# The first pair of tiles of a ConvFFN in direct block products, and a third room for split weights

## The chip, the cores and the metric

The kernel runs on one core of a Trainium2 chip. Its engines are called PE (matmuls), DVE, ACT and POOL (elementwise work) and SP, whose queue issues the transfers. The metric is the device time of one execution, in microseconds (us).

## What is computed

Two layers of a diffusion backbone over 1024 latent tokens and 256 context tokens of width 1024, in fp32. Each layer is a mixer (layer 0 a gated MLP beside a gated DeltaNet, layer 1 latent attention) and then a ConvFFN; only the latter concerns us. Layer 0 runs it on all 1280 tokens, layer 1 on the 1024 latent ones.

```python
def conv_ffn(h, w_up, conv_w, w_down):
    g, u = jnp.split(dwconv(h @ w_up, conv_w), 2, axis=-1)
    return (jax.nn.silu(g) * u) @ w_down
...
lat = lat + g2 * conv_ffn(modulate(rms_norm(lat, norm2_g[i]), sh2, sc2),
                          ffn_w_up[i], ffn_conv_w[i], ffn_w_down[i])
```

Here w_up is 1024 x 5632 and w_down 2816 x 1024.

## The kernel before

Every fp32 operand is split into a rounded part and a rest (h and l in the names): line 125 casts the rounded part on POOL, line 132 subtracts on DVE, and some operands are cast on ACT (line 123). A product of two split operands is three matmuls, h by h, h by l and l by h (lines 407 to 409 in `prod`, 588 to 590 in the down pass). A scheduler orders each engine's instructions when the kernel is built, on a timeline of its own; on the chip each engine takes them strictly in that order, with semaphore waits.

**The up pass** (`ffn_up`) goes over 22 pairs of tiles: tile ci of the gate columns and tile ci of the up columns of w_up, 128 wide each. The 1024 latent tokens make two halves of 512 columns, the width of 1024 two halves of four 128-row blocks. A pair is thus a 2 x 2 by 2 x 2 block product, and it is done in seven products of 12 matmuls with 512 columns (a scheme after Strassen and Winograd) in place of eight. They need B11 and B21 (the first token half), T1 (B12 - B11), B22, T2, T3 and T4 (sums of all four blocks), and S0 to S3, sums of weights that POOL makes (`sums`) and ACT and DVE split (`part`). `operands` makes the B and T blocks in two pieces of 256 columns (`ops[0]` and `ops[1]`). In layer 0 a pair also has 48 matmuls of 256 columns on the context tokens (`context`, bank upc).

The second token half comes late: its last 256 columns are normed (`last`) while the first pair runs. A norm takes squares, column sums on PE (nsum, line 195), their total (nall, line 216), an inverse root on ACT and DVE (from line 218), the scaling in place (xa), and then the operands of piece 1 (T1l, B22l, T2l and T4l on DVE, line 132). `begin[0]` and `begin[1]` put those steps into the program between the products of pair 0. `late` then gives up the memory of xa, and in layer 0 the sums S are made in it. `fill` (`ada1`, layer 0 alone) draws the next modulation's matmuls (ada, from weights adaw of 512 KB each) in between products.

Each pair ends with a convolution over tokens (`finish`, lines 630 and 632 on DVE), a SiLU on ACT, the product of both on POOL (line 496) and a store to DRAM (act<-y).

**The down pass** (`ffn_down`) goes over chunks of tokens (first one of 512, then three or two of 256), for each over two halves of the output and 11 pairs of w_down's blocks (`pr`; pairs count on through the pass as i, so pair 2 is the third). A pair is 24 matmuls with one split weight wdh, wdl. There are two rooms for these, and three for raw ones. After the matmuls of pair i the program asks for the split of pair i + 1 and the load of pair i + 2. The wh of a pair is written when PE has left its room. DVE also splits the down pass's moving operands (al), and works on the norm of the chunk before (the tail; `tail_rooms` holds its ten tiles).

## Time and profile before

| | us |
|---|---|
| median of 3 runs (lowest, highest) | 3308.62 (3308.61, 3311.64) |
| the profiled execution | 3311.97 |
| its span, first to last instruction | 3310.2 |
| PE busy | 3105.2 (94% of the span) |
| DVE, POOL, ACT busy | 2177.8, 1341.9, 1111.8 |
| up pass of layer 0, from its first product | 847.84 to about 1486 |
| down pass of layer 0 | about 1483 to 1815 |
| up pass of layer 1, from its first product | 2552.10 to about 3010 |
| down pass of layer 1 | about 3009 to 3297 |

PE's mean granted clock was 0.973 of full speed. In the page's 40 slices PE is at 9 tenths or more nearly everywhere; the slices at 8 or less hold the starts of stages. The chain of work that ended last covers a per cent or two of the span and so tells nothing here; the waits of PE by stage do.

### The profile page before, as it was taken

To read this page: it belongs to the slowest core of one execution; us is meant where nothing else is said; L and a number is where in the kernel's file an instruction comes from. 1 tells how busy PE (TensorE), PEld (TensorE's weight loads), DVE (VectorE), ACT (ScalarE), POOL (GpSimd) and SP (SyncE) were. 2 spreads that over 40 slices of the span, in tenths; PEclk is the share of its full clock that TensorE was granted. 3 is DMA by queue.
4 is the path that set the end of the run, shared out by engine and by line. 5 is a ranking of instruction groups with operands and counts; after the bars stand their busy time and mean duration, and the time that the engine had idled before them with its cause. 6 is when DMAs were issued, how large, how long until landed. Compare 5 with 4: busy or idle time off the path is not lost. (4 is left out here: it accounts for less than half of the span.)

```text
span 3310.2 us, 48558 instructions
## 1 busy us (share of the span) xinstructions
PE 3105.2 (94%) x18861; PEld 2587.9 (78%) x18861; DVE 2177.8 (66%) x3259; ACT 1111.8 (34%) x2144; POOL 1341.9 (41%) x1218
## 2 busy tenths in 40 slices
PE   7999899998599999999999999999998699999998
PEld 5667787886477788887899778988976577777887
DVE  6332876567765678885576456666657788887455
ACT  5322233333332333341111245555532333333110
POOL 4234323654533355442344232222135566664243
PEclk9999999999799999999999999999999899999999
DMA  7344946753235422144466231000034122225454
GB/s 250 121 141 133 300 134 207 237 152 120 74 121 163 154 97 74 68 151 158 139 223 216 73 104 47 27 22 22 8 128 153 46 82 77 77 83 197 159 192 146
DMA packets 257958, 419.80 MB, mean 127 GB/s; under 512 B 47024, under 2 KB 163968, under 8 KB 257600
## 3 DMA queue, kind: packets, MB, share of 16 engines
q1 hardware_dynamic: 257728, 416.70, 39.4%
q8 instruction: 149, 2.44, 0.3%
q14 instruction: 81, 0.66, 0.1%
HBM read 335.85 MB, written 80.78 MB: 126 GB/s over the span
## 5 line engine op out<-in xcount | busy, mean ns | idle before, releaser
L588 PE MATMUL dn<-ah,wdh 128*128 128x256 f32 (+1 forms) x1232 | 376.5, 317 | 3.8 <-POOL wdh L125 3.8
L589 PE MATMUL dn<-al,wdh 128*128 128x256 f32 (+1 forms) x1232 | 375.6, 316 | 0.0
L590 PE MATMUL dn<-ah,wdl 128*128 128x256 f32 (+1 forms) x1232 | 331.6, 321 | 22.8 <-DVE wdl L132 22.8
L125 POOL TENSOR_SCALAR wdh<-wdr 128x1024 fp32r<-128x1024 f32 x154 | 182.8, 1187 | 381.9 <-PE dn L589 323.0
L132 DVE TENSOR_TENSOR wdl<-wdr,wdh 128x1024 fp32r<-128x1024 f32 x154 | 196.6, 1280 | 193.6 <-POOL wdh L125 189.8
L125 POOL TENSOR_SCALAR wuh<-wur 128x1024 fp32r<-128x1024 f32 (+1 forms) x142 | 169.5, 1194 | 293.2 <-PE upc L408 118.5
L132 DVE TENSOR_TENSOR wul<-wur,wuh 128x1024 fp32r<-128x1024 f32 (+1 forms) x139 | 197.4, 1422 | 108.1 <-POOL wuh L125 107.7
L588 PEld LDWEIGHTS dn<-ah,wdh 128*128 128x128 f32 x1232 | 237.2, 192 | 23.8 <-issue 4.7
L590 PEld LDWEIGHTS dn<-ah,wdl 128*128 128x128 f32 x1232 | 214.7, 193 | 45.6 <-DVE wdl L132 27.4
L589 PEld LDWEIGHTS dn<-al,wdh 128*128 128x128 f32 x1232 | 236.9, 192 | 15.7 <-issue 0.8
L1675 POOL TENSOR_SCALAR p<-p,rsm 128x1280 f32<-128x1280 f32 x63 | 84.7, 1345 | 325.4 <-DVE rsm L1668 164.9
L630 DVE SCALAR_TENSOR_TENSOR y<-raw,fconv,y 128x1023 f32<-128x1023 f32 (+1 forms) x132 | 172.4, 1334 | 32.9 <-ACT y L419 32.6
L139 PE MATMUL proj<-hh,wih 128*128 128x512 f32 (+1 forms) x512 | 185.5, 364 | 0.0
L141 PE MATMUL proj<-hh,wil 128*128 128x512 f32 (+1 forms) x512 | 178.2, 348 | 1.3 <-DVE wil L132 1.3
L140 PE MATMUL proj<-hl,wih 128*128 128x512 f32 (+1 forms) x512 | 178.7, 350 | 0.6 <-DVE hl L253 0.6
L632 DVE SCALAR_TENSOR_TENSOR y<-raw,fconv,y 128x1023 f32<-128x1023 f32 (+1 forms) x132 | 175.6, 1353 | 0.1
L496 POOL TENSOR_TENSOR y<-y,y 128x1280 f32<-128x1280 f32 (+1 forms) x44 | 125.9, 2860 | 109.8 <-issue 61.9
L392 POOL TENSOR_TENSOR s<-wur 128x512 f32<-128x512 f32 x44 | 77.2, 1755 | 181.8 <-DMA wur<-in_w_up 122.1
L1657 DVE TENSOR_REDUCE mx<-sc 128x1 f32<-128x512 f32 (+1 forms) x192 | 114.6, 597 | 40.2 <-PE sc L1656 37.8
L419 ACT ACTIVATE y<-raw,fconv 128x1280 f32<-128x1280 f32 (+1 forms) x88 | 110.7, 1259 | 82.5 <-DVE raw L422 82.0
L110 ACT ACTIVATE p<-sc,nmx 128x512 f32<-128x512 f32 (+1 forms) x192 | 116.2, 617 | 49.1 <-DVE nmx L1661 48.9
L407 PE MATMUL upb<-T2h,S1h 128*128 128x512 f32 x176 | 70.2, 399 | 49.2 <-ACT S1h L123 26.6
(520 smaller groups left out, 9261.1 us busy)
## 6 DMA issues: line engine op xcount, KB each, us to landing
wdr<-in_w_down SPq DMA_DIRECT2D x154, 512.0 KB, 3.7
adaw<-in_ada_w SPq DMA_DIRECT2D x96, 512.0 KB, 4.1
wur<-in_w_up SPq DMA_DIRECT2D x88, 512.0 KB, 3.6
al<-act SPq DMA_DIRECT2D x20, 1024.0 KB, 6.7
t<-t SPq DMA_DIRECT2D x20, 768.0 KB, 6.3
act<-y SPq DMA_DIRECT2D x22, 640.0 KB, 3.0
wur<-in_w_out SPq DMA_DIRECT2D x24, 512.0 KB, 3.4
act<-y SPq DMA_DIRECT2D x22, 512.0 KB, 2.6
```

The source lines that it names most:

```text
L110: self.nc.scalar.activation(out, in_, func, **kw)
L125: nc.gpsimd.tensor_scalar(dst, src, 1.0, 0.0, op0=ALU.mult, op1=ALU.add)
L132: (self.nc.gpsimd if eng == "pools" else self.nc.vector).tensor_tensor(lo, src, f(hi), ALU.subtract)
L139: nc.tensor.matmul(ps, wh, xh, start=first and i == 0, stop=False)
L140: nc.tensor.matmul(ps, wh, xl, start=False, stop=False)
L141: nc.tensor.matmul(ps, wl, xh, start=False, stop=last and i == n - 1)
L496: nc.gpsimd.tensor_tensor(y[1], y[0], y[1], ALU.mult)
L588: nc.tensor.matmul(pss[o], wh[:, q, :], ah, start=pr == j == 0, stop=False)
L589: nc.tensor.matmul(pss[o], wh[:, q, :], al, start=False, stop=False)
L590: nc.tensor.matmul(pss[o], wl[:, q, :], ah, start=False, stop=pr == npr - 1 and j == 1)
L630: nc.vector.scalar_tensor_tensor(out=y[:, s0 + 1:e], in0=raw[:, s0:e - 1], scalar=w[:, 0:1], in1=y[:, s0 + 1:e], op0=ALU.mult, op1=ALU.add)
L632: nc.vector.scalar_tensor_tensor(out=y[:, s0:e - 1], in0=raw[:, s0 + 1:e], scalar=w[:, 2:3], in1=y[:, s0:e - 1], op0=ALU.mult, op1=ALU.add)
```

## The change

It has two parts, the same in both layers.

1. Pair 0 of the up pass is done without sums of weights. The first token half is W B11 + W B21, the second W B11 + W T1 + W B22, each for the gate and the up tile: 72 matmuls of 512 columns, and 96 of 256, since T1 and B22 are taken in their two pieces. The operand steps stand in three places (`begin[0]` to `begin[2]`), the norm's banks nsum and nall can be the single bank "a" (`ntag`), the weights of pair 1 are loaded at once, the sums and splits of pair 1's weights come right behind, and `fill` begins at pair 1, after one step in place of 16.
2. The down pass has a third room for split weights (pool `ffz`, pairs with i % 3 == 2) and asks for the split of pair i + 2 and the load of pair i + 3. `tail_rooms` has six tiles in place of ten, which makes the space. The pool is allocated after the up pass, behind `ffx`.

```diff
...
@@ -184,7 +185,7 @@

         nc = self.nc
         g = min(4, len(xs))
-        ps = self.bank("nsum")
+        ps = self.bank("nsum", self.ntag)
         last = {i % g: i for i in range(len(xs))}
         made = []

@@ -212,7 +213,7 @@
         part = tmp("pt")
         nc.vector.tensor_copy(part[:32 * g, :cn], ps[:32 * g, :cn])
         yield
-        ps2 = self.bank("nall")
+        ps2 = self.bank("nall", self.ntag)
         nc.tensor.matmul(ps2[:, :cn], self.ones[:32 * g, :], part[:32 * g, :cn], start=True, stop=True)
         m, r, t = tmp("m")[:, :cn], tmp("r")[:, :cn], tmp("t")[:, :cn]
         nc.vector.tensor_scalar(m, ps2[:, :cn], 1.0 / (32 * d), EPS, op0=ALU.mult, op1=ALU.add)
@@ -419,35 +420,76 @@
             nc.scalar.activation(y, raw, AF.Copy, scale=w[:, 1:2])
             self.conv_taps(y, raw, w, segs)

+        def gate(ci):
+
+            y = R["y"]
+            self.act(y[0], y[0], AF.Silu)
+            nc.gpsimd.tensor_tensor(y[1], y[0], y[1], ALU.mult)
+            nc.sync.dma_start(self.dr["a"][ci][:, :n], y[1])
+
+        def rows():
+            R["raw"] = [sp.tile([P, n], F32, tag=f"raw{i}", name=f"raw{i}") for i in range(2)]
+            R["y"] = [sp.tile([P, n], F32, tag=f"y{i}", name=f"y{i}") for i in range(2)]
+            raw = R["raw"]
+            return raw, raw[0][:, h1:h1 + 512], raw[1][:, h1:h1 + 512], v2(raw[0]), v2(raw[1])
+
         add = lambda o, a, b: nc.vector.tensor_tensor(o, a, b, ALU.add)
         B = self.B
+
+
+        steps, fill = fill, None
         load(0)
         weight(0, 0)
         weight(0, 1)
-        for ci in range(FT):
-            first = ci == 0
-            a, b, c, d = [None] * 4
+        load(1)
+        ps = [[self.bank("upa") for half in range(2)] for t in range(2)]
+        prod(ps[0][0], W[0], 0, B["B11"])
+        begin[0]()
+        prod(ps[0][1], W[1], 0, B["B11"])
+        for half in range(2):
+            prod(ps[0][half], W[half], 4, B["B21"], False)
+        for half in range(2):
+            prod(ps[1][half], W[half], 0, B["B11"])
+        e = self.bank("upc") if ctx else None
+        if ctx:
+            for half in range(2):
+                for k2 in range(2):
+                    context(e, half, k2)
+        for i in range(2):
+            cs = slice(256 * i, 256 * i + 256)
+            for half in range(2):
+                prod(ps[1][half][:, cs], W[half], 0, B["T1"], False, cs)
+                prod(ps[1][half][:, cs], W[half], 4, B["B22"], False, cs)
+            begin[1 + i]()
+        weight(1, 0)
+        R["sp"], sp = late()
+        sums(1)
+        for i in (1, 0, 2, 3):
+            part(1, i)
+        raw, g1, u1, g2, u2 = rows()
+        for half, (t1, t2) in enumerate(((g1, g2), (u1, u2))):
+            nc.scalar.copy(t1, ps[0][half])
+            nc.vector.tensor_copy(t2, two(ps[1][half]))
+            if ctx:
+                nc.scalar.copy(raw[half][:, :ctx], e[:, 256 * half:256 * half + 256])
+            finish(0, half)
+        weight(1, 1)
+        gate(0)
+        fill = steps
+        for ci in range(1, FT):
+            first = ci == 1
             e = self.bank("upc") if ctx else None
             a = self.bank("upa")
             prod(a, W[0], 0, B["B11"])
             if first:
-                begin[0]()
                 if ctx:
                     for half in range(2):
                         for k2 in range(2):
                             context(e, half, k2)
                 a2 = self.bank("up2")
                 prod(a2, W[0], 4, B["B21"])
-                begin[1]()
-                R["sp"], sp = late()
-                sums(0)
-                for i in (1, 0, 2, 3):
-                    part(0, i)
             load(ci + 1)
-            R["raw"] = [sp.tile([P, n], F32, tag=f"raw{i}", name=f"raw{i}") for i in range(2)]
-            R["y"] = [sp.tile([P, n], F32, tag=f"y{i}", name=f"y{i}") for i in range(2)]
-            raw, y = R["raw"], R["y"]
-            g1, u1, g2, u2 = raw[0][:, h1:h1 + 512], raw[1][:, h1:h1 + 512], v2(raw[0]), v2(raw[1])
+            raw, g1, u1, g2, u2 = rows()
             nc.scalar.copy(g1, a)
             if ctx and not first:
                 context(e, 0, 0)
@@ -492,9 +534,7 @@
                 weight(ci + 1, 1)
             else:
                 next(store, None)
-            self.act(y[0], y[0], AF.Silu)
-            nc.gpsimd.tensor_tensor(y[1], y[0], y[1], ALU.mult)
-            nc.sync.dma_start(self.dr["a"][ci][:, :n], y[1])
+            gate(ci)
         if fill is not None:
             drain(fill)
         sp.release()
@@ -518,7 +558,9 @@
         def weight(i):
             load(i)
             if i < total and i not in W:
-                W[i] = [wp.tile([P, KD, P], F32R, tag="wu" + a, name="wd" + a, bufs=2) for a in "hl"]
+
+                p, bufs = (wp, 2) if i % 3 < 2 else (self.ffz, 1)
+                W[i] = [p.tile([P, KD, P], F32R, tag="wu" + a, name="wd" + a, bufs=bufs) for a in "hl"]
                 self.split(*W[i], raws[i], "pool")

         def fetch(ch, gi):
@@ -570,6 +612,8 @@
             halve(0, 0)
             halve(0, 1)
             yield
+            weight(2)
+            load(3)
             todo = sequence()
             pend = iter(())
             i = 0
@@ -592,8 +636,8 @@
                             fn(*args)
                         raws.pop(i, None)
                         i += 1
-                        weight(i + 1)
-                        load(i + 2)
+                        weight(i + 2)
+                        load(i + 3)
                         if oh == 0:
                             next(pend, None)
                         elif pr in (2, 4, 6, 8):
@@ -612,8 +656,8 @@

     def tail_rooms(self, pool):

-        rs = [pool.tile([P, 512], F32, tag=f"t{i}", name=f"t{i}", bufs=1) for i in range(10)]
-        kinds = {"sq": rs[0:4], "h": rs[4:7], "pt": rs[7:8], "t": rs[7:8], "m": rs[8:9], "r": rs[9:10]}
+        rs = [pool.tile([P, 512], F32, tag=f"t{i}", name=f"t{i}", bufs=1) for i in range(6)]
+        kinds = {"sq": rs[0:4], "pt": rs[4:5], "m": rs[0:1], "t": rs[1:2], "r": rs[5:6], "h": rs[2:5]}
         cnt = {n: 0 for n in kinds}

         def get(name):
@@ -1913,6 +1957,7 @@
                                      for j in range(2)]), 1024, 256)

             def begin0():
+                self.ntag = "a"
                 for _ in range(8):
                     next(last)
                 for _ in range(4):
@@ -1920,18 +1965,19 @@

             def begin1():
                 drain(last)
-                for o in ops[1], ops[0]:
-                    for _ in range(7 if o is ops[1] else 3):
-                        next(o, None)
-                for o in ops[0], ops[1]:
+                self.ntag = "b"
+                for _ in range(3):
+                    next(ops[1])
+
+            def begin2():
+                for o in ops:
                     drain(o)

             m1 = {}
             sums = []

             def ada1():
-                for _ in range(16):
-                    yield
+                yield
                 yield from self.ada(ffw, "wur", 1, range(12), mp=lambda: sums[0], mtag="s0")
                 m1.update(sh1=self.modv(1, 0), gs1=self.gains(1, 1, ng[:, 2]), g1=self.modv(1, 2), sh2=self.modv(1, 3),
                           gs2=self.gains(1, 4, ng[:, 3]), g2=self.modv(1, 5))
@@ -1970,8 +2016,9 @@
                      [[("T3", 0, 8), ("T4", 8, 8), ("T2", 16, 6)]] * 3
             down = self.ffn_down(0, ffw, CHB, groups, None, load_x(CHB), lambda c0: g2[:, 1 if c0 < CTX else 0], tail0)
             self.ffn_up(0, ffw, NT, (512, lambda t: t.rearrange("p (s c) -> p s c", c=256)[:, 1:5:3, :]), [cseg, lseg], ada1(),
-                        (begin0, begin1), late, down)
+                        (begin0, begin1, begin2), late, down)
             xp.append(tc.alloc_tile_pool(name="ffx", bufs=1))
+            self.ffz = tc.alloc_tile_pool(name="ffz", bufs=1)
             tp = tc.alloc_tile_pool(name="fft", bufs=1)
             tmp = self.tail_rooms(tp)
             drain(down)
@@ -1979,6 +2026,7 @@
             get_in(0)
             early = self.mla_early(get_in, hv, self.pend)
             tp.release()
+            self.ffz.release()
             xp[0].release()
             hcx.release()

...
```

Three places show what the scheduler makes of it.

PE at the start of layer 0's up pass, before (B11, B21, T1 and so on are operands, CX the context, upa to upe banks; each "..." stands for more of the same product). Before:

```order
L407 MATMUL upa<-B11h,wuh 128x512
...
L195 MATMUL nsum<-nth,cst_66 32x256
L407 MATMUL upc<-CXh,wuh 128x256
...
L195 MATMUL nsum<-nth,cst_66 32x256 x3
...
L407 MATMUL up_8229<-B21h,wuh 128x512
...
L195 MATMUL nsum<-nth,cst_66 32x256 x4
L216 MATMUL nall<-nth,cst_66 128x256
L407 MATMUL upb<-T2h,S1h 128x512
```

And now:

```order
L408 MATMUL upa<-B11h,wuh 128x512
...
L196 MATMUL nsum<-nth,cst_66 32x256 x4
L410 MATMUL upa<-B21h,wul 128x512
...
L408 MATMUL upc<-CXh,wuh 128x256
...
L408 MATMUL upa<-T1h,wuh 128x256
...
L410 MATMUL upa<-B22h,wul 128x256
L196 MATMUL nsum<-nth,cst_66 32x256 x4
L217 MATMUL nall<-nth,cst_66 128x256
L299 MATMUL ada<-adaw,cst_64 32x256 x12
L408 MATMUL upa<-T1h,wuh 128x256 x2
```

Before the second nsum stand now 72 matmuls of 512 columns, the 48 of the context and the 48 of T1 and B22 in piece 0, where there were 24 of 512 and 48 of the context. What follows nall is three units of ada and then piece 1 of T1, in place of upb, which reads T2 and S1. In layer 1 the order is the same without the context and ada.

POOL at the start of layer 0's down pass, with the tiles' numbers and the semaphores waited for. Before (pairs 0 to 5 are split in the order of the rows; y1 is the last product of the up pass):

```order
L125 TENSOR_SCALAR wdh_12947<-wdr_12945 128x1024 [waits DMAHW6_49,PE_49,Pool_49]
L125 TENSOR_SCALAR wdh_13020<-wdr_12951 128x1024 [waits DMAHW0_49,PE_49,Pool_49]
L125 TENSOR_SCALAR wdh_13086<-wdr_13024 128x1024 [waits DMAHW1_49,DVE_49,PE_49]
L125 TENSOR_SCALAR wdh_13123<-wdr_13090 128x1024 [waits DMAHW2_49,DVE_49,PE_49]
L496 TENSOR_TENSOR y1_12863<-y0_12862,y1_12863 128x1280 [waits DMAHW4_49,DVE_49,Activation_49]
L125 TENSOR_SCALAR wdh_13153<-wdr_13127 128x1024 [waits DMAHW5_49,PE_49,Pool_49]
L125 TENSOR_SCALAR wdh_13190<-wdr_13157 128x1024 [waits DMAHW6_49,DVE_49,PE_49]
```

And now, with the first matmul of pair 2 on PE as the last row:

```order
L126 TENSOR_SCALAR wdh_13004<-wdr_13002 128x1024 [waits DMAHW6_49,PE_49,Pool_49]
L126 TENSOR_SCALAR wdh_13077<-wdr_13008 128x1024 [waits DMAHW0_49,PE_49,Pool_49]
L126 TENSOR_SCALAR wdh_13148<-wdr_13113 128x1024 [waits DMAHW1_49,DVE_49,PE_49]
L427 TENSOR_TENSOR y1_12920<-y0_12919,y1_12920 128x1280 [waits DMAHW4_49,DVE_49,Activation_49]
L126 TENSOR_SCALAR wdh_13185<-wdr_13152 128x1024 [waits DMAHW5_49,PE_49,Pool_49]
L126 TENSOR_SCALAR wdh_13109<-wdr_13081 128x1024 [waits DMAHW7_49,Pool_49]
L126 TENSOR_SCALAR wdh_13215<-wdr_13189 128x1024 [waits DMAHW6_49,DVE_49,PE_49]
L632 MATMUL dn_13117<-ah_13013,wdh_13109 128x512 [waits DMAHW3_49,DMAHW4_49,DMAHW1_49,DMAHW5_49,DMAHW0_49,DMAHW6_49,DVE_49,DMAHW7_49,Activation_49,Pool_49]
```

Pairs 0, 1, 2, 3, 4 and 5 are the tiles 13004, 13077, 13109, 13148, 13185 and 13215. Pair 2, whose room is the new one, is split after pairs 3 and 4 and after the last product y1, and its wait on DMAHW7 is for the store of that y1 to DRAM (the transfer whose end brings that semaphore to the count waited for).

POOL at the same place of layer 1, now:

```order
L427 TENSOR_TENSOR y1_26790<-y0_26789,y1_26790 128x1024 [waits DVE_49,DMAHW4_49,Activation_49,Pool_49]
L126 TENSOR_SCALAR wdh_27065<-wdr_27037 128x1024 [waits DMAHW7_49]
L126 TENSOR_SCALAR wdh_26989<-wdr_26987 128x1024 [waits DMAHW3_49,PE_49,Pool_49]
L126 TENSOR_SCALAR wdh_27033<-wdr_26993 128x1024 [waits DMAHW5_49,PE_49,Pool_49]
L126 TENSOR_SCALAR wdh_27104<-wdr_27069 128x1024 [waits DMAHW4_49,DVE_49,PE_49]
L126 TENSOR_SCALAR wdh_27141<-wdr_27108 128x1024 [waits DMAHW6_49,DVE_49,PE_49]
L427 TENSOR_TENSOR y1_26930<-y0_26929,y1_26930 128x1024 [waits DMAHW2_49,DVE_49,Activation_49]
```

Here pair 2 (27065) is split first of all, before pairs 0 and 1 (26989 and 27033), and waits for its own load alone; the last y1 of layer 1 is 26930.

## Rows read from the trace of the kernel before

**Rows 1.** PE's waits, 840 to 935: line waited for, total us, times, longest.

```profile
PE upb L407 <- ACT S1h L123: 26.6, 1, 26.6
PE nsum L195 <- ACT nth L207: 6.4, 1, 6.4
```

**Rows 2.** PE's waits, 2490 to 2640.

```profile
PE upb L407 <- POOL T2h L125: 22.6, 1, 22.6
```

**Rows 3.** PE's waits, down pass of layer 0, 1483 to 1816.

```profile
PE dn L590 <- DVE wdl L132: 15.5, 12, 3.6
PE dn L588 <- POOL wdh L125: 0.8, 2, 0.4
```

**Rows 4.** PE's waits, start of that pass, 1483 to 1525.

```profile
PE dn L590 <- DVE wdl L132: 3.0, 3, 2.3
```

**Rows 5.** PE's waits, down pass of layer 1, 3009 to 3300.

```profile
PE dn L590 <- DVE wdl L132: 7.3, 4, 2.5
PE dn L588 <- POOL wdh L125: 3.0, 1, 3.0
```

**Rows 6.** Stretches, PE: window, us, PE busy (count), granted clock, DMA share, GB/s.

```profile
898.00:904.00 6.00, 5.77 (x14) 0.51 0.32 117
904.00:942.00 38.00, 38.00 (x204) 1.00 0.25 75
1647.00:1651.00 4.00, 4.00 (x19) 0.50 0.49 131
3186.00:3195.00 9.00, 9.00 (x59) 0.74 0.92 299
```

**Rows 7.** Timeline, PE, up pass of layer 0: start us, us, line, op, tiles, count.

```profile
847.84 0.50 PE L407 MATMUL upa<-B11h,wuh 128*128 128x512 f32 x1
...
850.46 0.39 PE L409 MATMUL upa<-B11h,wul 128*128 128x512 f32 x1
...
863.36 0.28 PE L408 MATMUL upc<-CXl,wuh 128*128 128x256 f32 x1
...
866.70 0.28 PE L409 MATMUL upc<-CXh,wul 128*128 128x256 f32 x1
...
869.66 0.64 PE L195 MATMUL nsum<-nth,cst 128*32 128x256 f32 x8
...
942.23 0.50 PE L407 MATMUL upa<-B11h,wuh 128*128 128x512 f32 x1
```

**Rows 8.** Timeline, DVE, start of both up passes.

```profile
871.92 0.42 DVE L218 TENSOR_SCALAR nth<-nall 128x256 f32<-128x256 f32 x1
...
883.21 1.21 DVE L132 TENSOR_TENSOR T1l<-xa,T1h 128x1024 fp32r<-128x1024 f32 x1
...
2575.67 0.41 DVE L218 TENSOR_SCALAR nth<-nall 128x256 f32<-128x256 f32 x1
...
2587.06 1.21 DVE L132 TENSOR_TENSOR T1l<-xa,T1h 128x1024 fp32r<-128x1024 f32 x1
```

**Rows 9.** The page's DMA issues: count, KB each, median us to landing.

```profile
adaw<-in_ada_w SPq DMA_DIRECT2D x96, 512.0 KB, 4.1
```

**Rows 10.** Timeline, PE, up pass of layer 1.

```profile
2552.10 0.40 PE L407 MATMUL upa<-B11h,wuh 128*128 128x512 f32 x1
...
2630.18 0.39 PE L407 MATMUL upa<-B11h,wuh 128*128 128x512 f32 x1
```

**Rows 11.** Timeline, PE and POOL, start of layer 0's down pass.

```profile
1497.02 0.39 PE L588 MATMUL dn<-ah,wdh 128*128 128x512 f32 x1
...
1501.63 3.81 POOL L496 TENSOR_TENSOR y<-y,y 128x1280 f32<-128x1280 f32 x1 [1.60 <-ACT ah L123]
```

**Rows 12.** DMA issues, 1504 to 1510: KB each, median us to landing.

```profile
act<-y SPq DMA_DIRECT2D x1, 640.0 KB, 2.9
```

**Rows 13.** Line 125, the cast of wdh: ns min/median/max, first and last start.

```profile
L125 POOL TENSOR_SCALAR wdh<-wdr x154: 1046/1055/2986, 1477.9 to 3291.6; 128x1024 fp32r<-128x1024 f32 x154
```

**Rows 14.** Timeline, DVE, a burst in the down pass of layer 1.

```profile
3175.75 8.04 DVE L2045 SCALAR_TENSOR_TENSOR x<-x,norm_g,t 128x512 f32<-128x512 f32 x5
```

5 lines of the change are left out of this document (4 added, 1 removed).

## The prediction

> **What bounds the kernel now.** PE is busy for 94% of the span, so any time that the change can win is time in which PE stands still or runs at a lower clock, or work that PE no longer has. I read PE's waits stage by stage first, since the chain of waits covers too little of the span. Around the start of layer 0's up pass two waits stand out: 6.4 us for a norm's squares and 26.6 us for S1 [rows 1]; at the same place of layer 1 there are 22.6 us for T2 [rows 2]. In between, pair 0 cannot go on, because its third product already reads operands of the second token half, whose last 256 columns are normed only then. The down passes have many short waits for split weights: 16.3 us in layer 0 [rows 3], of which 3.0 fall at its start [rows 4], and 10.3 in layer 1 [rows 5]. Then the granted clock: behind a long wait PE's stretch of 6 us has 0.51, about the lower level of 1.2 GHz, and the 38 us after it the full 2.4 [rows 6]. So a long wait costs about 2.9 us more than itself, and behind the bursts of the down passes some of this shows too [rows 6].
>
> **Part 1, layer 0.** I work by places on the time axis of the profiled execution, from the first product of pair 0 at 847.84 to the first product of pair 2 at 942.23 [rows 7]; both versions have done pairs 0 and 1 and the same ada units by then. The prices: twelve products with 512 columns start within 2.62 us, thus 0.23 each, and of the 256-column ones 29 start within 3.34 us, thus 0.12 each [rows 7].
>
> In the new order 72 wide products (16.6), four nsum (0.6), 48 of the context (5.7) and 48 of T1 and B22 in piece 0 (5.7) stand ahead of the norm's second sum, which so starts at 876.4 in place of 869.66 [rows 7]. The norm of the last 256 columns is thus about 6.8 us later than before. Behind it the chain is the one of the trace: from the norm's step on line 218 at 871.92 to the end of T1l of piece 1 at 884.42 [rows 8]. With 6.8 us added, T1l is there at 891.2. PE waits for it from about 877.5 on; three ada units lie in this gap of 13.7 us. The second and the third load into a room that PE leaves in between, 4.1 us each [rows 9] and so 8.2, and cost nothing; if both took 7 us they would hold T1, since PE takes its order strictly. Then 48 narrow products, 6 us of them at half clock, take 8.7 us, to 899.9. Pair 1's split weights go into the rooms that these products leave: I allow a wait of 1.0, a little less than one subtraction of that size on DVE, 1.21 [rows 8]. Pair 1 itself, 84 wide and 48 narrow products, is 25.0 us. Pair 2 starts at 925.9, a gain of 16.3 us. What the change adds, 8.7 us of products (96 narrow for 12 wide), is in this. The convolution, SiLU and store of pair 0 now lie beside pair 1, as each pair's lie beside the next; the sums of pair 1's weights are made beside pair 1's first products, 11 us with the context; if that cover were gone, PE would wait for S1 as it did before, now in pair 1. Bounds for this term: 12, if the norm's steps are another 4 us late behind other work of DVE, and 19, if they are not later at all.
>
> **Part 1, layer 1.** Pair 0 starts at 2552.10 and pair 2 at 2630.18 [rows 10]. The second sum now comes at 2552.10 + 16.6 + 0.6 + 5.7 = 2575.0. Before, DVE did the step of line 218 only at 2575.67 [rows 8], with other work in its queue; now it can be done at about 2576.4. T1l ends 0.7 later than 2588.27 [rows 8], at 2589.0; 8.7 us of narrow products follow, then pair 1 with 84 wide ones (19.3), whose first products need nothing that is later. Pair 2 starts at 2617.0, a gain of 13.2, between 9 and 15.
>
> **Part 2, start of layer 0's down pass.** Here the order says something the diff doesn't: pair 2's split stands on POOL behind the last product y1 and the split of pair 4, and waits for y1's store, since its room lies where y1 lay. Before, PE began pair 2 at 1497.02, and y1's product ran on POOL from 1501.63 to 1505.44 [rows 11]; the store lands 2.9 us later [rows 12], at 1508.4. The cast is then 1.05 us at the least [rows 13], with some time beside it taken by DVE; I take 1.2. PE can begin pair 2 at 1509.6: a new wait of 12.6 us, and 2.9 of half clock behind it. Everything in PE's queue stands behind it, but nothing of DVE's or POOL's is late thereby; on SP the store stands behind the loads of pairs 3 to 5, whose rooms are free by then. The loads that the change asks for a pair earlier have the same count and size. The 3.0 us of waits at the start [rows 4] go, since pairs 3 and 4 are split meanwhile. Net 12.5 lost; at least 9, if the y chain gets ahead by what it no longer shares, and 16 with a slow store. In layer 1 pair 2 is split first and this wait does not exist.
>
> **Part 2, the bursts.** DVE takes work in long series, one of 8.04 us [rows 14], and the split behind it comes late. With the third room PE can hold one more pair, 24 narrow products or 2.86 us. Most of the later waits are shorter than this (3.6 the longest), and go. Of layer 0's 16.3 - 3.0 = 13.3, with 2.0 us lost to the clock behind the longest wait [rows 6], I leave 3 us, because some bursts follow each other: 12.3 gained. Of layer 1's 10.3, with 9 us at 0.74 behind the longest burst (2.3) [rows 6], I leave 3.3 for that burst, since three pairs (8.6 us) less the time to split one do not span 8.04 and a split: 9.3 gained. Each between half and all. The smaller set of tail rooms costs nothing by the order: h takes tiles whose squares have been summed before.
>
> **Sum.** 16.3 + 13.2 - 12.5 + 12.3 + 9.3 = 38.6 us off the profiled execution of 3312.0. That one is 3.4 above the median of the runs, so I take the same off the median: 3308.6 - 38.6 = 3270.0.
>
> **Rivals.**
> *A, the reserve does not come back.* A pair's split takes 1.05 us on POOL [rows 13] and then 1.21 on DVE [rows 8], 2.26 of the 2.86 us that PE needs for a narrow pair. If the splits of neighbouring pairs cannot overlap, the reserve grows by 0.6 per pair and needs five pairs to grow by one; bursts that follow sooner meet an empty third room. At the worst nothing of the 12.3 and the 9.3 is gained: 3291.6, and half of that, 3280.8, is as likely. For it: a cast on POOL takes 1.055 in the median and up to 2.986 [rows 13]. Against it: a pair of the first chunk is wide and takes twice as long, and most of the waits stand alone.
> The Trainium skill (SBUF — State Buffer, "SBUF: two separate sides") has such a rule: DVE and GpSimd share a pair of ports as a lock, and one that meets an instruction of the other with two SBUF inputs is held for its whole length. By that rule A would be the likelier; the trace agrees in direction, with casts between 1.05 and 2.99 us.
> *B, pair 2 is not late.* If y1's product and store come earlier by the time that I give to the wait, the 15.5 us are not paid: 3254.5. Against it: y1 hangs on DVE's convolution, which the change leaves where it was.
> *C, the first part doesn't do what it says.* The operands come early in piece 0 alone; piece 1 still has the whole chain. If that chain is held by the new work (three ada transfers ahead of T1 in PE's queue, pair 1's splits on DVE), half of the 29.5 us stays: 3284.8.
> *D, slower: the clock.* The narrow products start right out of a wait of 13 us, in both layers. If the lower level then lasted not 6 us but through pair 1, layer 0 would run 30.7 us of work in twice that, 27.8 more than I count, and layer 1 25.0, 22.1 more: 3270 + 49.9 = 3319.9. It decides from 38.6 us lost, some 77 us of products at half clock. Against it: behind the 26.6 us wait, the clock was back after 6 us [rows 6], and the narrow products are as dense as wide ones.
>
> **Chances and range.** My forecast 0.60, A 0.14, B 0.10, C 0.10, D 0.06. The range runs from B to nearly the worst of A: 3253 to 3290; outside it are D and the ends of the others. A measurement of this kernel can tell 0.2%, some 6.6 us, from no change. Faster by more than that are the forecast, A, B and most of C: 0.90. Within 0.2%: 0.04, from C with A; slower: 0.06, from D.
>
> **What would show it.** In the profile of the changed kernel: no wait for S1 or T2 in pair 0, but one of about 13 us for T1l in each layer, with a granted clock near 0.5 for 6 us behind it; pair 2 of the up pass some 16 and 13 us earlier; one wait of about 12 us of a line of the down pass for POOL's wdh at the start of layer 0's pass and none in layer 1; the sum of the other waits for splits below 8 us in both passes. I am wrong in the first part if T1l's wait is 20 us or more; in the second, if the new wait is missing, or the waits later in the passes stand as they did.

## The result, and the profile after

The changed kernel takes 3285.72 us in the median of 4 runs (3285.19 to 3290.97), beside 3310.13 for the kernel before on the same chip (4 runs, 3308.61 to 3312.68): ratio 0.9928, 95% interval 0.9916 to 0.994, thus 24.4 us faster. The forecast was 3270.0, with a range from 3253 to 3290. The sign and the places are as foretold, and the sum is 14 us too large. The profiled execution has a span of 3283.5 us against 3310.2. The places on the time axis, read from PE's timelines, show where the 26.7 us come from:

| place on PE | before | after | earlier by |
|---|---|---|---|
| first product of layer 0's up pass | 847.84 | 846.82 | 1.0 |
| first product of layer 0's down pass | 1483.24 | 1468.82 | 14.4 |
| first product with 256 columns there | 1611.41 | 1609.24 | 2.2 |
| last product there | 1828.33 | 1822.57 | 5.8 |
| first product of layer 1's up pass | 2552.10 | 2544.65 | 7.5 |
| first product of layer 1's down pass | 3025.49 | 3010.67 | 14.8 |
| first product with 256 columns there | 3152.71 | 3132.93 | 19.8 |
| last product there | 3297.09 | 3269.70 | 27.4 |

The differences between neighbouring rows are the terms of the sum:

| term | forecast | measured |
|---|---|---|
| layer 0, pairs 0 and 1 | 16.3 | 13.4 |
| layer 1, pairs 0 and 1 | 13.2 | 7.4 |
| layer 0's down pass, first chunk (the new wait) | -12.5 | -12.3 |
| layer 0's down pass, narrow chunks (bursts) | 12.3 | 3.6 |
| layer 1's down pass | 9.3 | 12.6 |

They add up to 24.7; the other 2.0 lie ahead of layer 0's up pass (1.0), between the layers (1.7) and in the tail (-0.7), which the change does not touch. (By these places the kernel before ends its down pass of layer 0 at 1828 us and begins that of layer 1 at 3025, not at about 1815 and 3009 as the table ahead has it; the waits of [rows 3] and [rows 5] are the same by either.)

**Layer 0's up pass.** PE's waits from 840 to 935 in the profile after, which answer to [rows 1]:

```profile
PE ada L299 <- DMA adaw<-in_ada_w: 7.6, 2, 3.8
PE wo L142 <- DVE wul L133: 2.2, 1, 2.2
PE upa L409 <- DVE T1l L133: 1.1, 1, 1.1
PE up L408 <- ACT raw L471: 0.8, 1, 0.8
```

The 26.6 us for S1 and the 6.4 for a square are gone. PE now waits for T1 of piece 1, and the two loads of ada fall within that wait, 3.8 us each, as the prediction had it; T1l comes 1.1 us behind the last of them. The DVE rows that answer to [rows 8], the norm's step and T1l:

```profile
879.26 0.42 DVE L219 TENSOR_SCALAR nth<-nall 128x256 f32<-128x256 f32 x1 [0.79 <-PE nall L217]
...
890.65 1.21 DVE L133 TENSOR_TENSOR T1l<-xa,T1h 128x1024 fp32r<-128x1024 f32 x1
```

The granted clock, in windows (length, busy time of PE, PEld, DVE, ACT and POOL, then the clock, the share of DMA, GB/s):

```profile
847.00:850.00 3.00, 3.00 (x8) 2.33 (x8) 1.71 (x3) 1.20 (x3) 0.00 (x0) 0.50 1.14 379
885.00:892.00 7.00, 2.08 (x15) 0.79 (x11) 6.06 (x7) 3.66 (x6) 2.87 (x2) 0.50 0.41 99
892.00:898.00 6.00, 6.00 (x29) 6.00 (x30) 5.02 (x5) 0.00 (x0) 2.65 (x2) 0.51 0.15 61
898.00:904.00 6.00, 4.46 (x28) 3.47 (x27) 6.00 (x5) 1.63 (x4) 5.64 (x4) 1.00 0.00 0
```

Behind the wait for T1 there are 6 us at 0.51, the lower level of 1.2 GHz, as in [rows 6]. The first row was not foretold: pair 0 itself starts at 0.50, behind the wait of 2.2 us for an output projection's weights (the row of wo above). This is not so in every execution: c1_both below has the same wait of 2.2 us, and a clock of 1.00 behind it:

```profile
849.00:852.00 3.00, 3.00 (x14) 2.46 (x14) 1.72 (x3) 1.18 (x3) 0.00 (x0) 1.00 1.02 373
```

**Layer 0's down pass.** The wait that replaces [rows 4], in PE's timeline (start, length, instruction, and in brackets the idle time before it with its cause):

```profile
1496.41 0.79 PE L632 MATMUL dn<-ah,wdh 128*128 128x512 f32 x1 [12.39 <-POOL wdh L126]
```

POOL's timeline ahead of it has y1's product, the cast of pair 4 and that of pair 2:

```profile
1487.21 5.00 POOL L427 TENSOR_TENSOR y<-y,y 128x1280 f32<-128x1280 f32 x1 [8.25 <-ACT ah L124]
1492.18 1.04 POOL L126 TENSOR_SCALAR wdh<-wdr 128x1024 fp32r<-128x1024 f32 x1
1495.31 1.05 POOL L126 TENSOR_SCALAR wdh<-wdr 128x1024 fp32r<-128x1024 f32 x1 [2.08 <-DMA act<-y]
```

Pair 2's cast waits for the store of y1 (act<-y) and PE for the cast: 12.39 us, where 12.6 had been worked out. PE's later waits in the pass, 1500 to 1823, which answer to [rows 3]:

```profile
PE dn L634 <- DVE wdl L133: 7.1, 7, 2.8
PE dn L632 <- DVE x L649: 1.9, 1, 1.9
PE dn L632 <- POOL wdh L126: 0.5, 1, 0.5
```

What POOL's casts waited for a load in the narrow chunks, in the profile before:

```profile
POOL wdh L125 <- DMA wdr<-in_w_down: 13.3, 7, 3.2
```

And in the profile after:

```profile
POOL wdh L126 <- DMA wdr<-in_w_down: 34.7, 21, 4.5
```

9.5 us of short waits stay where 3 were expected (13.3 before). One is of a new kind: PE stands 1.9 us for DVE's x, that is for a bank. And the casts wait for loads 21 times in place of 7.

**Layer 1.** PE's waits at the start of the up pass, 2544 to 2700, which answer to [rows 2]:

```profile
PE upa L408 <- ACT T1h L124: 8.4, 1, 8.4
PE upa L409 <- DVE T1l L133: 3.4, 1, 3.4
PE upd L408 <- DVE raw L436: 2.7, 3, 1.9
PE upa L408 <- POOL wuh L126: 0.8, 1, 0.8
```

The only wait for a split in the down pass, which answers to [rows 5]:

```profile
PE dn L634 <- DVE wdl L133: 3.0, 1, 3.0
```

PE waits 11.8 us for T1 where it waited 22.6 for T2. Behind it stand two waits that the prediction did not have, for POOL's cast of pair 1's weights (0.8) and for DVE's raw (1.9 the longest).

### The profile page after: what moved, and what is told of

It is laid out like the page before. It is cut to its first block, busy times and chain, and to the rows that moved or that the text cites. A ratio compares the mean times of both kernels' runs of the same rounds, so it can differ in the third digit from the quotient of the medians.

```text
span 3283.5 us, 48865 instructions
## 1 busy us (share of the span) xinstructions
PE 3116.2 (95%) x19029; PEld 2604.8 (79%) x19029; DVE 2180.9 (66%) x3245; ACT 1105.7 (34%) x2136; POOL 1340.1 (41%) x1210
## 5 line engine op out<-in xcount | busy, mean ns | idle before, releaser
L632 PE MATMUL dn<-ah,wdh 128*128 128x256 f32 (+1 forms) x1232 | 391.1, 319 | 15.0 <-POOL wdh L126 12.9
L634 PE MATMUL dn<-ah,wdl 128*128 128x256 f32 (+1 forms) x1232 | 385.5, 319 | 11.2 <-DVE wdl L133 11.1
L633 PE MATMUL dn<-al,wdh 128*128 128x256 f32 (+1 forms) x1232 | 388.7, 317 | 0.0
L126 POOL TENSOR_SCALAR wdh<-wdr 128x1024 fp32r<-128x1024 f32 x154 | 192.1, 1249 | 345.7 <-PE dn L633 222.2
L634 PEld LDWEIGHTS dn<-ah,wdl 128*128 128x128 f32 x1232 | 234.9, 193 | 30.3 <-DVE wdl L133 13.8
L674 DVE SCALAR_TENSOR_TENSOR y<-raw,fconv,y 128x1023 f32<-128x1023 f32 (+1 forms) x132 | 171.1, 1324 | 35.2 <-ACT y L420 34.9
L676 DVE SCALAR_TENSOR_TENSOR y<-raw,fconv,y 128x1023 f32<-128x1023 f32 (+1 forms) x132 | 187.6, 1443 | 0.1
L133 DVE TENSOR_TENSOR pl<-pt,ph 128x512 fp32r<-128x512 f32 (+1 forms) x192 | 108.8, 593 | 8.1 <-ACT ph L124 7.5
```

The lines of the kernel that those rows point to most:

```text
L126: nc.gpsimd.tensor_scalar(dst, src, 1.0, 0.0, op0=ALU.mult, op1=ALU.add)
L133: (self.nc.gpsimd if eng == "pools" else self.nc.vector).tensor_tensor(lo, src, f(hi), ALU.subtract)
L632: nc.tensor.matmul(pss[o], wh[:, q, :], ah, start=pr == j == 0, stop=False)
L633: nc.tensor.matmul(pss[o], wh[:, q, :], al, start=False, stop=False)
L634: nc.tensor.matmul(pss[o], wl[:, q, :], ah, start=False, stop=pr == npr - 1 and j == 1)
L674: nc.vector.scalar_tensor_tensor(out=y[:, s0 + 1:e], in0=raw[:, s0:e - 1], scalar=w[:, 0:1], in1=y[:, s0 + 1:e], op0=ALU.mult, op1=ALU.add)
```

## The experiments

My theory after this reading: the first part is worth what the table says, and its limit is that PE, strictly in order, comes late to the second norm sum; the new wait is the room alone; the reserve of the third room is used up in layer 0, for a reason still open. Rivals for that: POOL's casts, late loads, or DVE's long series itself. All ratios are to the kernel before on the same chip, with 95% intervals. The scheduler orders every version anew, so an edit can also move instructions that it doesn't name, or none at all; where this bears on a reading, it is said.

**1. Each part alone** (e1_direct_only, e2_rooms_only). The first leaves the direct products and takes back the rooms; the second is the reverse.

```diff
-                p, bufs = (wp, 2) if i % 3 < 2 else (self.ffz, 1)
-                W[i] = [p.tile([P, KD, P], F32R, tag="wu" + a, name="wd" + a, bufs=bufs) for a in "hl"]
+                W[i] = [wp.tile([P, KD, P], F32R, tag="wu" + a, name="wd" + a, bufs=2) for a in "hl"]
...
-                        weight(i + 2)
-                        load(i + 3)
+                        weight(i + 1)
+                        load(i + 2)
```

> The first part alone: eight direct block products for pair 0, but two rooms for the down pass's split weights as before. My account of the changed kernel by stages says that the first part gives all of 1.0 + 13.4 us in layer 0, 7.4 in layer 1 and 1.7 in between, and that the third room takes 8.7 in layer 0 and gives 12.6 in layer 1. So this kernel should be 20 to 24 us faster than the kernel before (ratio about 0.993), its down pass of layer 0 should last 345 us from the first to the last product as before, with 16 us of short waits, and that of layer 1 some 271 to 272. Rival: the two parts need each other, since waits of the down pass move when the up pass ends earlier; then the down passes differ by over 3 us from those of the kernel before.

> The second part alone: three rooms and the smaller set of tail rooms, with pair 0 as before. By the stage account this is worth 12.6 in layer 1 less 8.7 in layer 0: 4 us faster (ratio 0.998 to 1.0), with one wait of 10 to 15 us for wdh in pair 2 of layer 0's down pass, and none like it in layer 1. Rival: the wait for y1's store is due to the earlier end of the up pass (y1 comes 14 us earlier there, but so does PE); then it is missing here or below 6 us, and the kernel is 12 us or more faster.

Measured: 0.9944 (0.9931 to 0.9957) and 0.9983 (0.9974 to 0.9993), thus by the ratios 18.5 and 5.6 us faster, together what the whole change gives. The first is a little under what was expected. In the first the down passes last 344.9 and 269.2 us (345.1 and 271.6 before). Its narrow chunks of layer 0 take 219.1 us and those of the kernel before 216.9, though every engine there has the same instructions in the same order: 2 us in such a stage, from one profile to another, show nothing. In the second the wait stands in the same place with the same length, so it has nothing to do with the earlier end of the up pass; its row, on PE from 1484 to 1624:

```profile
PE dn L591 <- POOL wdh L125: 12.4, 1, 12.4
```

Its narrow chunks take 213.2 us in layer 0, and layer 1's down pass 257.9, much as in the changed kernel (213.3 and 259.0). The parts add.

**2. The third room elsewhere** (e3_room_elsewhere).

```diff
-            xp.append(tc.alloc_tile_pool(name="ffx", bufs=1))
             self.ffz = tc.alloc_tile_pool(name="ffz", bufs=1)
+            xp.append(tc.alloc_tile_pool(name="ffx", bufs=1))
```

> The changed kernel with the third room of layer 0 allocated ahead of the tiles x, so that it lies where the up pass's sums lay and not where y1 lay. By my theory the wait of 12.4 us in pair 2 and the half clock behind it go, and the old 3.0 us of waits do not come back: the first chunk of layer 0's down pass lasts 125 to 128 us in place of 140.4, and the kernel is 12 to 15 us faster than the changed kernel (about 3272, ratio to the kernel before about 0.9885). Rival: PE stops at pair 2 or soon behind it for something else that comes at the same time (the last halves of a, whose tiles come by the same store, or x, which now lies where y1 lay); then a wait of 6 us or more stands in the first chunk and the gain is below 7.

Measured: 0.9903 (0.9887 to 0.9919). The first chunk lasts 125.9 us in place of 140.4, and this is all that PE waits in it, from 1470 to 1600:

```profile
PE dn L634 <- DVE wdl L133: 1.6, 1, 1.6
```

The room was the whole cause. By the ratios the kernel gains 8 us on the changed kernel and not 12 to 15; in its profile layer 1's up pass is 3.0 us longer (a further wait of 3.4 for DVE's raw, in pair 2), the stretch between the layers 2.0, and pair 0 of layer 0 starts 1.7 later. The edit's lines touch none of this, but in layer 1's up pass the scheduler's order of a few instructions on PE and DVE is another.

**3. The second sum first** (e4_sum_first).

```diff
+        begin[1]()
         e = self.bank("upc") if ctx else None
...
-            begin[1 + i]()
+            if i:
+                begin[2]()
```

> The changed kernel with the second sum of the norm issued ahead of the context and of T1 and B22 in piece 0. My account says that T1 of piece 1 is late in both layers only because PE, which takes its products in order, comes to the sum behind those 96 (layer 1: 48) narrow products, though its squares are there at about 866 (layer 1: 2557). Then the sum starts at 866 to 868 in place of 877.25 and at about 2562 in place of 2568.35, T1l is there 8 to 10 and 5 to 6 us earlier, and the kernel is 12 to 16 us faster than the changed kernel (about 3271). Rival: T1l is held by DVE, whose other work fills the time, or pair 1 waits in turn for its weights; then the wait for T1 shrinks, but others grow, and the gain is below 6.

Measured: 0.9895 (0.9881 to 0.9908), 11 us faster than the changed kernel by the ratios. In layer 0 the sum starts at 866.83, T1l at 883.55 in place of 890.65, and the up pass is 8.1 us shorter. Layer 1 gains 0.8 only. PE's waits there, 2536 to 2690:

```profile
PE upd L408 <- DVE raw L436: 5.9, 2, 3.4
PE upa L408 <- ACT T1h L124: 5.6, 1, 5.6
PE upa L409 <- DVE T1l L133: 3.4, 1, 3.4
PE upa L408 <- POOL wuh L126: 1.3, 1, 1.3
```

T1h's wait fell from 8.4 to 5.6, those for raw rose from 2.7 to 5.9. The rise is not the work of the earlier sum, though. In the run of experiment 2, where the sum stands as in the changed kernel, PE waits as long for raw (2533 to 2700):

```profile
PE upd L408 <- DVE raw L436: 6.3, 3, 3.4
```

The order of DVE, ACT and POOL in layer 1's up pass is the same in these two runs, and that of PE differs by the place of the sum alone. From the one to the other T1l is there 3.5 us sooner after the first product, and the pass falls from 469.0 to 465.2 us. So the theory holds in layer 0, and in layer 1 at a smaller size: 3.8 us on a like order, where T1l was to come 5 to 6 earlier. The rival, that the earlier T1 only makes other waits grow, is not shown.

**4. Both, and four ways to the short waits** (c1_both, then e5 to e8, each an edit of c1_both).

> The changed kernel with the third room elsewhere and the second sum first, both at once. The two savings lie in different stages, so they add: the first chunk of layer 0's down pass lasts 126 us in place of 140.4, layer 0's up pass 614 in place of 622, layer 1's up pass 465 to 469 (there DVE's work takes most of it back, as in the run of the sum alone). Some 22 us faster than the changed kernel, about 3263 (ratio 0.985 to 0.987). Rival: the earlier T1 only moves a wait to pair 2, and the two together give under 15. The narrow chunks of layer 0 stay at 212 to 214 us with 9 to 12 us of short waits, which is what the next three runs start from.

Measured: 0.9861 (0.9845 to 0.9877), 22 us faster than the changed kernel: up pass 613.0, first chunk 129.0 (126 expected; a wait of 3.2 us for wdl stands in it), narrow chunks 213.0. On this base, the casts on ACT (e5_act_casts):

```diff
-                self.split(*W[i], raws[i], "pool")
+                self.split(*W[i], raws[i], "act")
```

> The last kernel with the casts of the down passes' weights on ACT, not POOL. It tests whether the short waits of layer 0's narrow chunks (9 to 12 us) come from POOL: from casts that last up to 3 us beside DVE's work, or stand behind the tail's work in POOL's queue. By that account the waits fall below 5 us and the narrow chunks of layer 0 last 206 to 209 us in place of 213. By the account that DVE itself is full there (it is busy without a gap for 30 us while the tail's work of the first chunk is done), or that loads are late, nothing changes: 211 to 215, or it gets worse by some us, where a cast stands behind ACT's own work for the tail.

Measured: 0.981 (0.9797 to 0.9823), 16 us faster than c1_both. Layer 0's narrow chunks last 200.3 us in place of 213.0 (206 to 209 expected), layer 1's 131.2 in place of 135.6, and PE's waits from 1590 to 1790 are 2.8 in place of 11.3. Groups of instructions in that stretch (busy time, mean ns of one, idle time before them and its causes), for c1_both:

```profile
L126 POOL TENSOR_SCALAR wdh<-wdr 128x1024 fp32r<-128x1024 f32 x62 | 83.8, 1355 | 81.9 <-DMA wdr<-in_w_down 44.6 <-PE dn L635 25.0 <-DVE al L133 6.4
L133 DVE TENSOR_TENSOR wdl<-wdr,wdh 128x1024 fp32r<-128x1024 f32 x61 | 83.8, 1383 | 37.7 <-POOL wdh L126 35.8 <-PE nsum L196 1.8
...
L133 DVE TENSOR_TENSOR al<-al,ah 128x512 fp32r<-128x512 f32 x22 | 20.9, 991 | 6.0 <-ACT ah L124 6.0
...
L252 DVE SCALAR_TENSOR_TENSOR t<-x,gs,t 128x512 f32<-128x512 f32 x6 | 7.5, 1277 | 0.0
...
L254 DVE SCALAR_TENSOR_TENSOR h3l<-t,mv,h3h 128x512 fp32r<-128x512 f32 x3 | 4.9, 1665 | 0.0
```

The same groups with the casts on ACT:

```profile
L133 DVE TENSOR_TENSOR wdl<-wdr,wdh 128x1024 fp32r<-128x1024 f32 x64 | 81.0, 1271 | 51.4 <-ACT wdh L124 49.2 <-PE nsum L196 1.7
...
L124 ACT ACTIVATE wdh<-wdr 128x1024 fp32r<-128x1024 f32 x64 | 67.3, 1056 | 72.6 <-PE dn L635 52.4 <-DMA wdr<-in_w_down 18.0 <-issue 1.3
L133 DVE TENSOR_TENSOR al<-al,ah 128x512 fp32r<-128x512 f32 x22 | 14.0, 685 | 5.3 <-ACT ah L124 5.3
...
L252 DVE SCALAR_TENSOR_TENSOR t<-x,gs,t 128x512 f32<-128x512 f32 x6 | 6.4, 1080 | 0.0
...
L254 DVE SCALAR_TENSOR_TENSOR h3l<-t,mv,h3h 128x512 fp32r<-128x512 f32 x3 | 2.5, 858 | 0.0
```

The same DVE instructions take 685 ns in place of 991 and 858 in place of 1665, and a cast takes 1056 on ACT and 1355 on POOL. The trace of c1_both shows that it is the overlap: of its 22 subtractions al, the 15 that run beside an instruction of POOL take 1135 ns in the mean and the 7 others 684; a cast beside one of DVE takes 1436 and alone 1049. (The 858 still has POOL's other work beside two of the three; alone such a block takes 741.) DVE's 30 us without a gap were thus no fixed amount of work: part of it was instructions held up beside POOL's. Over the narrow chunks DVE is busy 134.5 us in place of 157.6 with the same 159 instructions, and its longest series is 22 us.

The spread of the tail (e7_spread) was to test the rival that the series as such is the cause.

```diff
-            if mid and k == KD // 2:
+            if k and (steps or mid and k == KD // 2):
                 yield
...
```

> The kernel with both, with the tail of layer 0's down pass given out in smaller pieces: one of the eight blocks of a normed chunk a pair, over the next chunk's both halves, in place of all eight behind one pair. DVE has the same work, but over 22 pairs in place of some 10. By the account that DVE's 30 us without a gap use up the reserve, most of the waits in layer 0's narrow chunks go (12 to below 5 us; narrow chunks 205 to 208 us), and layer 1, whose tail has no such blocks, stays as it is. By the accounts of POOL's casts or late loads, under 2 us. A loss is open too: the squares of the next chunk then stand between the blocks, and the last blocks come late for the next stage.

Measured: 0.9856 (0.9842 to 0.9871); the narrow chunks take 213.9 us. But nothing was spread: the scheduler made the same order out of it, and in the two traces PE, DVE, ACT and POOL each have the same instructions in the same order from the first to the last. DVE's series stands where it stood; a window in it, for c1_both (columns as above):

```profile
1615.20:1644.20 29.00, 24.78 (x202) 23.96 (x201) 28.97 (x26) 6.73 (x11) 19.91 (x14) 1.00 0.44 137
```

The same for e7_spread:

```profile
1615.20:1644.20 29.00, 26.01 (x201) 25.40 (x201) 28.96 (x26) 6.74 (x11) 20.92 (x14) 0.94 0.46 137
```

So the run is a second measurement of c1_both (3265.55 and 3266.71 us), and whether the clumping matters stays untested.

The loads (e6_four_loads; the tail has four tiles in place of six):

```diff
+                q, t, k = (wp, "wur", 3) if i % 4 < 3 else (self.ffz, "wr4", 1)
-                raws[i] = wp.tile([P, KD, P], F32, tag="wur", name="wdr", bufs=3)
+                raws[i] = q.tile([P, KD, P], F32, tag=t, name="wdr", bufs=k)
```

> The kernel with both, with a fourth room for the loads of the down pass's weights, filled one pair earlier; the tail's rooms are four in place of six to make the space. It tests whether the reserve of the third room is not rebuilt because a load can start only when the split three pairs before has left its room: a load of 4.2 us, a cast of 1.05 and a subtraction of 1.2 in three rooms make 2.2 us a pair at the best, against 2.86 that PE takes, and POOL's casts waited for loads 21 times for 34.7 us in the changed kernel (8 times for 17.7 before). By that account layer 0's narrow chunks gain 4 to 8 us (205 to 209). By the account that DVE is full, under 2 us, or a loss of a few us if the tail misses its rooms.

Measured: 0.9839 (0.9826 to 0.9852); the narrow chunks take 206.8 us, 6.2 less, and POOL's casts wait for loads 9.4 us where the row of c1_both above has 44.6. The same group from 1590 to 1790:

```profile
L126 POOL TENSOR_SCALAR wdh<-wdr 128x1024 fp32r<-128x1024 f32 x64 | 86.0, 1347 | 77.5 <-PE dn L636 56.6 <-DMA wdr<-in_w_down 9.4 <-DVE al L133 6.7
```

So late loads are a part of it too; a room is free for the next load only when the split of its last content is done, and that is held up. With both edits (c2_all):

> The casts on ACT and the fourth room for loads together. With the casts on ACT only 2.8 us of waits for splits are left in layer 0's narrow chunks, and ACT waits for loads there for 18 us. If loads are what is left, the narrow chunks end at 197 to 199 us in place of 200.3, and the kernel is 2 to 5 us faster than the one with the casts on ACT (about 3247). If it was POOL alone, the fourth room adds nothing (within 2 us), since the 6 us that it gave beside casts on POOL were cover for the same delay.

Measured: 0.9793 (0.9777 to 0.9809); narrow chunks 198.4 us. The two gains, 12.7 and 6.2, do not add: 14.6 together, so in part they shorten the same delay. Last, two rooms again with the casts on ACT (e8_two_rooms_act, the diff of experiment 1, but with the six tiles of the tail):

> The kernel with the casts on ACT, but with two rooms for the split weights of the down passes as in the kernel before. With the casts on POOL the third room gave layer 0's narrow chunks 3.6 us (216.9 to 213.3), and the casts on ACT gave them 12.7 more (213.0 to 200.3). If a reserve of one more pair is what matters once it is rebuilt quickly, it needs the third room: two rooms then give 207 us or more. If the waits came from DVE's and POOL's instructions, which take up to twice as long beside each other (DVE's blocks of the norm 1.66 in place of 0.74 us), there are few bursts left, and two rooms give 201 to 205; the third room is then worth under 5 us in layer 0 and about as much in layer 1.

Measured: 0.9852 (0.9835 to 0.9868); layer 0's narrow chunks take 206.5 us, layer 1's 140.7 (200.3 and 131.2 with three rooms). 206.5 lies between what the two accounts expected. With the runs so far, layer 0's narrow chunks and PE's waits in them are these:

| | casts on POOL | casts on ACT |
|---|---|---|
| two rooms | 216.9 and 219.1 us (before, e1_direct_only), waits of 13.3 and 12.9 | 206.5 us, 6.8 |
| three rooms | 212.5 to 213.9 us (six profiles), 9.5 in the changed kernel | 200.3 us, 2.8 |

The casts on ACT give 10 to 14 us with either number of rooms. The room gives 3 to 6.6 us beside casts on POOL and 6.2 beside casts on ACT; that it is worth more beside quick casts is not shown.

**5. The same elsewhere** (e9_up_casts_act, then c3_out_casts_act): the casts of the up passes' weights on ACT, then those of the output projections too.

```diff
-                self.split(*W[half], raws[ci, half], "pool")
+                self.split(*W[half], raws[ci, half], "act")
```

> The same with the casts of the up passes' weights on ACT too. It asks whether what the first part lost in layer 1 (waits of 1.9 to 3.5 us for DVE's raw in pairs 1 and 2, and 0.8 to 1.4 for POOL's cast of pair 1's weights) comes from DVE and POOL beside each other. If so, the raw waits and that for the cast go, and layer 1's up pass is 3 to 6 us shorter (454 to 457 in place of 459.5), layer 0's 1 to 3. If DVE is late by its own amount of work, nothing changes; if the casts stand behind ACT's copies and sums' splits in its queue, PE waits for ACT once a pair, 22 times in each pass, and the kernel is 10 us or more slower.

Measured: 0.9734 (0.9719 to 0.9748), 20 us faster than c2_all by medians. Layer 0's up pass is 1.1 us shorter and layer 1's 13.4 (451.5 in place of 464.9), where 3 to 6 were expected: not only the waits of pair 1 go, but the short ones for raw in later pairs too. (The scheduler's order in layer 1's first pairs is another as well, and a wait of 2.6 for raw stays in pair 2.) From layer 0's last down product to layer 1's first it takes 1175.3 us in place of 1188.2. (Of the rest 5.8 lie ahead of layer 0's up pass, where the edit changes nothing, and 4.2 in the first chunk of its down pass.) The gain is spread over the whole up pass of layer 1. A window of 200 us in its middle, for c2_all (columns as above):

```profile
2650.00:2850.00 200.00, 196.15 (x843) 157.14 (x842) 169.38 (x150) 68.46 (x90) 128.88 (x71) 1.00 0.24 79
```

The like for e9_up_casts_act:

```profile
2635.00:2835.00 200.00, 200.00 (x871) 163.18 (x870) 179.02 (x156) 91.62 (x113) 113.26 (x53) 1.00 0.25 82
```

DVE's subtractions for the split weights in the window of c2_all:

```profile
L133 DVE TENSOR_TENSOR wul<-wur,wuh 128x1024 fp32r<-128x1024 f32 x20 | 35.2, 1761 | 22.0 <-POOL wuh L126 22.0
```

And in that of e9_up_casts_act:

```profile
L133 DVE TENSOR_TENSOR wul<-wur,wuh 128x1024 fp32r<-128x1024 f32 x20 | 35.4, 1771 | 5.6 <-ACT wuh L124 5.6
```

PE runs 871 matmuls there in place of 843. Here DVE's instruction has the same mean (1761 and 1771 ns), but waits 5.6 us for the cast in place of 22.0: here it is POOL's queue that made DVE late, and DVE that made PE wait (3.8 us in the first window for DVE's raw, nothing in the second).

```diff
-                get = self.stream(ffw, w_half1 * 3, [P, KD, P], "wu", "pool", 3, n=4)
+                get = self.stream(ffw, w_half1 * 3, [P, KD, P], "wu", "act", 3, n=4)
...
-                              lambda i: "pools" if i < 3 else "pool", 3)
+                              lambda i: "pools" if i < 3 else "act", 3)
```

> The last kernel with the casts of the output projections' weights, ahead of each ConvFFN, on ACT as well. There PE waits 9.8 us (layer 0) and 10.6 us (layer 1) for these weights' casts on POOL and their subtractions on DVE, and the last such wait, 2.2 us in the changed kernel, leaves pair 0 of layer 0 at a granted clock of 0.50 for its first 3 us, which was the first error in my sum. If POOL's queue and the pairing with DVE are the cause, both sums of waits fall below 6 us, pair 0 starts at the full clock, and the kernel is 8 to 14 us faster (3213 to 3219). If DVE is late by its own work there (it is busy 53 of 60 us ahead of layer 1's pass), the waits keep their size and only change their name, and the time is within 4 us; if the casts stand behind ACT's squares and y's splits, it is slower by up to 10.

Measured: 3215.57 us, 0.9695 (0.9682 to 0.9708), 11 us faster than e9 and the fastest version of this study. PE's waits ahead of layer 1's up pass, 2430 to 2525:

```profile
PE wo L140 <- ACT wuh L124: 3.0, 1, 3.0
PE wo L142 <- DVE wul L133: 2.5, 1, 2.5
```

There they fall from 10.6 to 5.5 us. Ahead of layer 0's up pass, from some 65 us before its first product on, these are the waits of e9 (780 to 847):

```profile
PE wo L142 <- DVE wul L133: 5.3, 5, 2.4
PE wo L140 <- POOL wuh L126: 4.5, 6, 1.8
```

And those of c3 (780 to 844):

```profile
PE wo L142 <- DVE wul L133: 2.6, 4, 1.1
PE wo L140 <- ACT wuh L124: 2.2, 3, 1.3
```

They fall from 9.8 to 4.8, so both sums are below 6 as expected. Pair 0 of layer 0 starts at a clock of 1.00, but it did so in the profile of e9 too, where the last wait for weights was 0.9, and in c1_both, where it was 2.2 as in the changed kernel; so this point was not decided by the edit.

## Why the prediction was right, and where not

- **Layer 0, pairs 0 and 1** (16.3, measured 13.4): the mechanism and the gap were right. The first product to the end of T1l takes 45.0 us where 43.4 were worked out, as pair 0 starts at half clock in this profile, which the sum left out; 3 us at 0.50 cost 1.5. Pair 1 takes 28.4 us and not 25.0: a fourth ada unit, where the sum had the same units in both versions, waits of 0.8 for ACT's raw and 0.6 for DVE's wul, and products at 0.232 in place of 0.23 us. At the first product of pair 2, to which the sum was worked out, the gain is 12.4; the pass as a whole, which has one ada unit less behind that place, gains the 13.4.
- **Layer 1** (13.2, measured 7.4): the mis-sized step is pair 1, "whose first products need nothing that is later". T1l is 1.3 late, and then come the waits for wuh (0.8) and raw (1.9), the latter with 1.7 us lost to the clock behind it (0.84 over 10.7 us). Experiment 5 shows that the waits for wuh and raw in pair 1 hang on the casts of weights in POOL's queue, since they are gone with these on ACT (and an order that is another in places); the prediction looked at PE's operands and not at what POOL and DVE had left to do for pairs 0 and 1.
- **The start of layer 0's down pass** (-12.5, measured -12.3): right in place, cause and size; experiments 1 and 2 confirm that it is the room.
- **The bursts** were the step that failed in layer 0: "Most of the later waits are shorter than this (3.6 the longest), and go", with at least half of the 12.3 as the bound. 3.6 came. Rival A, with 0.14, described it: the reserve does not come back, since the cast on POOL and the subtraction on DVE take longer beside each other. Its row [rows 13] already had casts of 2.986. Experiment 4 shows this for the casts, and the late loads as a second part that neither the forecast nor A had. It does not show what the close order of DVE's series adds, since the spread did not take place. The rule of the Trainium skill on which A leaned (SBUF — State Buffer, "SBUF: two separate sides") agrees in direction: in c1_both DVE's blocks of the norm with two inputs take 741 ns alone, and 1545 to 1665 in the mean beside POOL's instructions. In **layer 1's down pass** the same term came out larger (9.3, measured 12.6): 7.3 of its 10.3 us of waits went, and PE is busy 5.4 us less (255.9 in place of 261.3), at a mean granted clock of 0.99 in place of 0.97.
- B and D did not come: the new wait is there, and the clock was back 6 us behind the wait for T1. C, half of the first part, is not the whole (20.8 of 29.5 came), but in layer 1, with 7.4 of 13.2, it is near the truth, by POOL's and DVE's queues and not by ada. That the measured total lies 1 us from C's 3284.8 is chance: 8.7 of the 14 us are missing in the bursts, which C counts in full, and the 3.3 more in layer 1's down pass cover a part.

## What to carry to other kernels

A spare buffer need not take away the short waits of its consumer: here the third room gave layer 0's narrow chunks 3 to 6.6 us, where 13 us of waits stood, and quicker producers gave 10 to 14 with or without it. Before counting on a buffer, add up the cast, the subtraction and the load of a unit at the durations that they have beside each other, not at their least, and compare the sum with the consumer's time. Where casts on one engine and two-input instructions on another meet all the time, and a third engine is idle, moving the casts may be worth more than the buffer. Where a reordering removes a wait, look at what the engine behind it (here DVE) still has in its queue, and look where a new room lies in memory. Where a scheduler makes the order, see in the traces that an edit changed it before a result without a gain is read as an answer: e7_spread moved nothing.

## What the runs showed that I had not expected

- Moving the casts of split weights from POOL to ACT, one word in four places, took about 47 us off (c1_both 3266.71 to c3_out_casts_act 3215.57, less the 4.5 us from e5_act_casts to c2_all, which are the fourth room's), more than the change itself.
- A block of the norm on DVE, 512 columns with two inputs, takes 1545 to 1665 ns in the mean beside POOL's instructions and 741 alone; the cast itself takes 1436 on POOL beside DVE's instructions, 1049 alone, and 1056 on ACT.
- Behind a wait of 2.2 us, with other short ones ahead of it, pair 0 started at a granted clock of 0.50 for 3 us in the changed kernel, and at 1.00 in e1_direct_only and c1_both, which have the same wait. Where that wait was 0.9 (e9_up_casts_act) it started at 1.00.
- Profiles of one and the same order of instructions in layer 0's narrow chunks differ there by 0.9 us (c1_both, e7_spread) and by 2.2 (before, e1_direct_only).
